# The first row of a diffusion-transformer layer on both DMA queues: when it is loaded, and what stands behind it

## The chip, the cores and the metric

The kernel runs on one core of a Trainium2 chip. Its time is the device time of one execution in microseconds (us); a run's number is compared as the median of several executions. Five engines work side by side, each in its own order and held together by semaphores: TensorE (PE: matmuls, with PEld for the loading of weights), VectorE (DVE), ScalarE (ACT), GpSimd (POOL) and SyncE (SP). SyncE and ScalarE issue nearly all transfers, each on a queue of its own (q1 and q10 in the profile).

## What is computed

One layer of a diffusion transformer on 1024 latent tokens of 1024 channels, with 256 context tokens. It begins by making the modulation from the condition vector c, and the projections read the modulated tokens:

```python
mod = jax.nn.silu(c) @ w_mod + b_mod          # 6 x 1024: shift, scale, gate for two sublayers
h   = x * (1 + scale) + shift                 # modulated latent tokens
proj = h @ w_in + b_in                        # queries, keys, values of two attentions, and gates
mixed = (sigmoid(g_a) * (o_a @ w_a) + sigmoid(g_b) * (o_b @ w_b)) @ w_out
```

The context tokens are modulated in the same way from a constant vector c_ctx. Windowed attention, global attention, the merge above and a convolutional feed-forward network follow. Everything is float32.

## The kernel before

A float32 matmul is made of three. `split` writes an operand as a high part (rounded, by ScalarE, line 80) and a low part (the difference, line 85, by VectorE or GpSimd), and `mm3` adds high times high (L88), high times low (L89 or L90) and low times high. For a weight w the parts are called wh and wl. `wsplit(wr, nm, le)` makes both from a raw weight tile; `le` names the engine of the low part. "q1acc" are eight accumulators of the first stage, "accqa" four of a later one.

The program is written as one sequence; a scheduler places each engine's instructions in an order that follows priorities and its own estimate of when their inputs are ready. So an edit in one place can change the order on engines elsewhere. Tiles come from rings of buffers: the raw weights have three, the split weights eight, and the large tiles of 128 x 1024 share 19 slots H0 to H18, handed out in turn by `ht` and given back by `hput`; a load into a slot waits until the one who used it before is done. Transfers signal one of eight completion semaphores in turn, so a ninth transfer waits for the first to land.

The first stage makes one set of queries. Before it, `spread(sc, c_row, 0)` broadcasts the row of c to 128 partitions (512 KB in a tile "row") and applies SiLU, giving `sc`. For each of eight k, `load1(k)` issues two tiles of modulation weights (wm, 512 KB each), a weight tile wr (256 KB) and a tile of x (xr, 512 KB) on SyncE's queue. `modulate(k)` splits the weight (whqb, wlqb), reduces each wm tile against sc on VectorE (`mod`, line 186, into a column of modc), and makes the modulated tokens hh (high) and hl (low). 24 matmuls per k follow: eight accumulators times three.

After the stage come, on TensorE, three gates g0 to g2 (48 matmuls each; their weights wg are split by ScalarE and GpSimd into whg and wlg), and then accqa: eight k of 12 matmuls with the weights wqa, split by ScalarE (whqa) and VectorE (wlqa). Between them VectorE does rotary embedding and norms for the queries of the first stage (rt1q, rt2q, Q, and the reduction of squares cvt<-sqq), and 48 further columns of modulation: each is one tile "wml" (512 KB, L648) reduced by line 186. wml47 is the first of these, then 46, 45 and so on; the first 16 use `scc`, the SiLU of the context's row, the others sc. The sigmoids of the gates leave through tiles sg (L666) and transfers on ScalarE's queue (L667); these tiles share the H slots with wml.

Of the kernel before, what the change touches and what calls it, by code (L numbers as in the profile page):

```python
# [13 lines left out]
P = 128  # L14
D = 1024
T = 1024
# [11 lines left out]
HALF = 512  # L28
# [39 lines left out]
def layer_kernel(  # L68
# [6 lines left out]
    nc = tc.nc  # L75
    PSUM = bass.MemoryType.PSUM

    def split(src, hi, lo, hi_eng, lo_eng):
        if hi_eng is nc.scalar:
            nc.scalar.copy(hi, src)  # L80
        elif hi_eng is nc.gpsimd:
            nc.gpsimd.tensor_scalar(out=hi, in0=src, scalar1=1.0, scalar2=0.0, op0=ALU.mult, op1=ALU.add)  # L82
        else:
            hi_eng.tensor_copy(hi, src)
        lo_eng.tensor_tensor(out=lo, in0=src, in1=hi.bitcast(F32), op=ALU.subtract)  # L85

    def mm3(ps, a, b, start, stop, resumed=False):
        nc.tensor.matmul(ps, a[0], b[0], start=start, stop=False, skip_group_check=resumed)  # L88
        nc.tensor.matmul(ps, a[0], b[1], start=False, stop=False, skip_group_check=resumed)  # L89
        nc.tensor.matmul(ps, a[1], b[0], start=False, stop=stop, skip_group_check=resumed)  # L90
# [3 lines left out]
    def ctile(shape, dt, name):  # L94
        return const.tile(shape, dt, tag=name, name=name)
# [2 lines left out]
    identr = ctile([P, P], R32, "identr")  # L98
    modc = ctile([P, 48], F32, "modc")
    bmc = ctile([P, 48], F32, "bmc")  # L100
    nc.scalar.dma_start(bmc, bmod)
    modx = ctile([P, 16], F32, "modx")
    negsink = ctile([P, 8], F32, "negsink")
    sinkb = ctile([P, 8], F32, "sinkb")
# [26 lines left out]
    def ht(name, shape=(P, T), dt=F32):  # L131
        hslot[name] = pool, tag = hfree.pop(0)
        return pool.tile(list(shape), dt, tag=tag, name=name, bufs=1)

    def hput(*names):
        for n in names:
            hfree.append(hslot.pop(n))
# [18 lines left out]
    def raw(name):  # L156
        return ph1.tile([P, 512], F32, tag="raw", name=name, bufs=RAWB)

    def wsplit(wr, nm, le="vector"):
        wh = ph1.tile([P, 512], R32, tag="wp", name=f"wh{nm}", bufs=8)  # L160
        wl = ph1.tile([P, 512], R32, tag="wp", name=f"wl{nm}", bufs=8)
        split(wr, wh, wl, nc.scalar, getattr(nc, le))
        return wh, wl
# [7 lines left out]

    sc, scc = ht("sc"), ht("scc")

    def spread(dst, src, n):
        row = ht(f"row{n}")
        hput(f"row{n}")
        nc.scalar.dma_start(row, src.partition_broadcast(P))
        nc.scalar.activation(dst, row, AF.Silu)

    def tmp(name):  # L180
        t = ht(name)
        hput(name)
        return t

    def mod(w, row, bias, o):
        nc.vector.tensor_tensor_reduce(out=w, in0=w, in1=row, scale=1.0, scalar=bias, op0=ALU.mult, op1=ALU.add,  # L186
                                       accum_out=o)
# [5 lines left out]
    def load1(k):  # L193
        wm = []
        for j in (0, 1):
            w = tmp(f"wm{j}_{k}")
            nc.sync.dma_start(w, wmodT[j * 8 + k])
            wm.append(w)
        x = tmp(f"xr{k}")
        wr = raw(f"wr{k}")  # L200
        nc.sync.dma_start(wr, w_qb[k])
        nc.sync.dma_start(x, xT[k])
        st1[k] = wm, x, wr

    def modulate(k):
        wm, x, wr = st1.pop(k)
        w = wsplit(wr, f"qb{k}")
        for j in (0, 1):
            col = j * 8 + k
            mod(wm[j], sc, bmc[:, col:col + 1], modc[:, col:col + 1])  # L210
        hh = hTp.tile([P, T], R32, tag="hT", name=f"hh{k}", bufs=16)
        hl = hTp.tile([P, T], R32, tag="hT", name=f"hl{k}", bufs=16)
        a, b = modc[:, k:k + 1], modc[:, 8 + k:9 + k]
        for s in [slice(0, HALF), slice(HALF, T)] if k == 0 else [slice(0, T)]:
            nc.scalar.activation(hh[:, s], x[:, s], AF.Identity, bias=a, scale=b)
            nc.scalar.activation(x[:, s], x[:, s], AF.Identity, bias=a, scale=b)
            nc.vector.tensor_tensor(out=hl[:, s], in0=x[:, s], in1=hh[:, s].bitcast(F32), op=ALU.subtract)
        hT.append((hh, hl))
        return w

    spread(sc, c_row, 0)
    load1(0)
    nc.vector.tensor_scalar(out=bmc[:, 8:16], in0=bmc[:, 8:16], scalar1=1.0, scalar2=None, op0=ALU.add)
    for k in (1, 2):
        load1(k)
    acc = [acc_tile(f"q1acc{t}") for t in range(NT)]
    w = modulate(0)
    for k in range(KT):
        if k == 2:
            spread(scc, cc_row, 1)  # L230
        if k + 3 < KT:
            load1(k + 3)
        wn = modulate(k + 1) if k + 1 < KT else None
        for t in range(NT):
            s = slice(t * P, (t + 1) * P)
            mm3(acc[t], (hT[k][0][:, s], hT[k][1][:, s]), w, k == 0, k == KT - 1)
        w = wn
# [461 lines left out]
    for n, (gi, k) in enumerate(order):  # L699
# [9 lines left out]
        nm, src, tiles = groups[gi]  # L709
# [3 lines left out]
        w, c = ready.pop((gi, k))  # L713
        for t in tiles:
            if t < NT:
                s = slice(t * P, (t + 1) * P)
                a = hT[k][0][:, s], hT[k][1][:, s]
            else:
                s = slice((t - NT) * P, (t - NT + 1) * P)
# [222 lines left out]
    for f in range(2, KT):  # L942
        bT[1, f] = ht(f"bT1_{f}")
        nc.sync.dma_start(bT[1, f], sgd[KT + f])
        w = wb[f // 2]
        ps = big(f"b1_{f}")
        for j in range(4):
            k = (f % 2) * 4 + j
# [588 lines left out]
    s = LN2_S[-1]  # L1537
    w = s.stop - s.start
# [207 lines left out]
```

## Time and profile before

| | |
|---|---|
| runs of the kernel (us) | 1590.85, 1590.62, 1592.18; median 1590.85 |
| profiled execution | 1593.3 us, of which the span is 1591.5 |
| mean granted clock of TensorE | 0.993 |
| TensorE busy | 1537.1 us (97%) |
| VectorE, ScalarE, GpSimd busy | 1181.3, 813.3, 730.1 us |
| traffic | 230.00 MB, mean 145 GB/s |

One execution is recorded instruction by instruction. A row of a timeline gives start, duration, engine, line, operation, "out<-in" by tile names, and in brackets how long the engine was idle before and what released it. A table of waits gives the total, the count and the longest. A row of a window gives for each engine the busy time in it, then the granted clock, the share of the DMA engines that was busy, and GB/s.

### The profile page before, as it was taken

How to read it: one execution, taken by the hardware profiler on the slowest of the kernel's cores; microseconds unless marked ns; L12 is line 12 of the kernel's file. 1: busy time of each engine (PE TensorE's matmuls, PEld its weight loads, DVE VectorE, ACT ScalarE, POOL GpSimd, SP SyncE). 2: the span in 40 equal slices, each digit the busy share in tenths (PEclk: the TensorE clock that was granted, in tenths of full speed). 3: DMA queues.
4: the chain of work that ended last, by engine and by line, in shares of the span. 5: the costliest groups of instructions: out<-in, count | busy, mean ns of one | idle time of the engine just before them, and what ended most of it. 6: DMA issues, size and time to landing. Idle time of an engine off the chain costs nothing.

```text
span 1591.5 us, 22189 instructions
## 1 busy us (share of the span) xinstructions
PE 1537.1 (97%) x7748; PEld 1278.4 (80%) x7748; DVE 1181.3 (74%) x1768; ACT 813.3 (51%) x1450; POOL 730.1 (46%) x727
## 2 busy tenths in 40 slices
PE   6999999999999999999999999999999999999997
PEld 5878788878886887777688888888888888888887
DVE  7797646628888777888674778788888788657884
ACT  5422122448888667688521564454444444535552
POOL 0573212426666556665422453566667665021021
PEclk9999999999999999999999999999999999999999
DMA  9685663322227555532451222333334446996731
GB/s 379 218 309 177 214 204 101 118 79 74 64 81 178 136 127 127 125 84 41 141 173 65 80 80 93 106 106 106 106 106 108 117 116 175 368 274 202 260 107 54
DMA packets 112368, 230.00 MB, mean 145 GB/s; under 512 B 12960, under 2 KB 27808, under 8 KB 112160
## 3 DMA queue, kind: packets, MB, share of 16 engines
q1 hardware_dynamic: 96816, 198.93, 37.9%
q0 software_dynamic: 10400, 20.19, 8.3%
q10 hardware_dynamic: 5040, 9.46, 1.6%
q8 instruction: 61, 1.00, 0.3%
q14 instruction: 51, 0.42, 0.1%
HBM read 177.35 MB, written 65.86 MB: 153 GB/s over the span
## 4 chain that ended last, share of the span: by engine, by line
PE 76%; DVE 8%; DMA 7%; ACT 4%; issue 3%; POOL 2%; SPq 0%; DVEq 0%; ACTq 0%; POOLq 0%
PE ptr L529 4%; PE p L89 3%; PE p L88 3%; PE p L90 3%; PE b L90 3%; PE b L89 3%; PE b L88 3%; PE g L88 2%; PE g L89 2%; PE g L90 2%; PE d L89 2%; PE c L89 2%; PE a L89 2%; PE c L90 2%; PE a L90 2%
## 5 line engine op out<-in xcount | busy, mean ns | idle before, releaser
L539 DVE TENSOR_TENSOR ptl<-ptr,pth 128x512 fp32r<-128x512 f32 x188 | 124.7, 685 | 28.2 <-ACT pth L538 25.8
L529 PE MATMUL ptr<-ident,p 128*128 128x128 f32 x816 | 126.6, 278 | 9.5 <-DVE ptl L539 6.9
L538 ACT CAST pth<-ptr 128x512 fp32r<-128x512 f32 x188 | 106.6, 588 | 56.3 <-PE ptr L529 32.6
L85 DVE TENSOR_TENSOR ld<-rd,hd 128x1024 fp32r<-128x1024 f32 x77 | 94.8, 1249 | 50.8 <-ACT hd L80 48.7
L424 ACT ACTIVATE p<-p,nm 128x1024 f32<-128x1024 f32 (+2 forms) x128 | 125.3, 981 | 11.2 <-DVE p L457 10.5
L529 PEld LDWEIGHTS ptr<-ident,p 128*128 128x128 f32 x816 | 93.7, 140 | 39.8 <-DVE ptl L539 13.5
L80 ACT CAST hd<-rd 128x1024 fp32r<-128x1024 f32 x77 | 79.4, 1049 | 81.9 <-PE p L90 55.5
L550 PE MATMUL av<-pth,VT 128*128 128x512 f32 x236 | 104.6, 443 | 1.0 <-ACT avs L556 0.5
L88 PE MATMUL p<-hd 128*128 128x512 f32 x264 | 103.2, 391 | 0.0
L89 PE MATMUL p<-ld,hd 128*128 128x512 f32 x264 | 102.8, 390 | 0.2 <-DVE ld L85 0.2
L90 PE MATMUL p<-hd,ld 128*128 128x512 f32 x264 | 102.7, 389 | 0.0
L88 PE MATMUL g<-hh,whg 128*128 128x512 f32 x256 | 99.9, 390 | 0.0
L90 PE MATMUL g<-hh,wlg 128*128 128x512 f32 x256 | 99.7, 389 | 0.0
L89 PE MATMUL g<-hl,whg 128*128 128x512 f32 x256 | 99.6, 389 | 0.0
L551 PE MATMUL av<-ptl,VT 128*128 128x512 f32 x236 | 97.6, 414 | 2.0 <-POOL ptl L85 1.9
L85 POOL TENSOR_TENSOR wlg<-wg,whg 128x512 fp32r<-128x512 f32 x32 | 45.5, 1428 | 113.3 <-ACT whg L80 83.1
L457 DVE TENSOR_SCALAR_CACHE_REDUCE p<-s,cvt,nmc 128x1024 f32<-128x1024 f32 x64 | 84.5, 1340 | 12.3 <-PE s L413 11.8
L412 PE MATMUL s<-KL,q 128*128 128x512 f32 (+2 forms) x192 | 76.0, 396 | 2.9 <-ACT p_x L424 2.0
L186 DVE CUSTOM_DVE_ANT_0 wml<-wml,sc,bmc 128x1024 f32<-128x1024 f32 x32 | 44.6, 1406 | 43.0 <-DMA wml<-in_wmodT_dram 40.0
L413 PE MATMUL s<-KL,q 128*128 128x512 f32 (+2 forms) x192 | 71.7, 373 | 0.0
L82 POOL TENSOR_SCALAR pth<-prw 128x512 fp32r<-128x512 f32 x48 | 31.1, 648 | 87.6 <-ACT prw L535 62.1
L80 ACT CAST wS<-s 128x512 fp32r<-128x512 f32 x76 | 45.5, 621 | 45.6 <-POOL s L1077 42.8
(420 smaller groups left out, 4959.4 us busy)
## 6 DMA issues: line engine op xcount, KB each, us to landing
wml<-in_wmodT_dram SPq DMA_DIRECT2D x48, 512.0 KB
ru<-in_w_up_dram SPq DMA_DIRECT2D x38, 512.0 KB
rd<-td SPq DMA_DIRECT2D x55, 256.0 KB
rd<-sd SPq DMA_DIRECT2D x44, 256.0 KB
rd<-in_w_dn_dram SPq DMA_DIRECT2D x33, 256.0 KB
wm<-in_wmodT_dram SPq DMA_DIRECT2D x16, 512.0 KB
wg<-in_w_g_dram SPq DMA_DIRECT2D x32, 256.0 KB
sgd<-sg ACTq DMA_DIRECT2D x32, 256.0 KB
```

What stands on the lines that cost most here:

```text
L80: nc.scalar.copy(hi, src)
L85: lo_eng.tensor_tensor(out=lo, in0=src, in1=hi.bitcast(F32), op=ALU.subtract)
L88: nc.tensor.matmul(ps, a[0], b[0], start=start, stop=False, skip_group_check=resumed)
L89: nc.tensor.matmul(ps, a[0], b[1], start=False, stop=False, skip_group_check=resumed)
L90: nc.tensor.matmul(ps, a[1], b[0], start=False, stop=stop, skip_group_check=resumed)
L424: nc.scalar.activation(p, s, AF.Exp, bias=nm[:, h:h + 1], scale=scale, accum_out=sm[:, h:h + 1])
L457: nc.vector.tensor_scalar(out=p, in0=o, scalar1=self.qscale(nqs)[:, hs] if self.br else -1.0, scalar2=self.other[:, hs], op0=ALU.mult, op1 ...
L529: nc.tensor.transpose(tr[:, h * P:(h + 1) * P], self.pslice(h, n), ident)
L538: nc.scalar.copy(hi, tr)
L539: nc.vector.tensor_tensor(out=lo, in0=tr, in1=hi.bitcast(F32), op=ALU.subtract)
L550: nc.tensor.matmul(self.av, v, hi, start=first, stop=False)
L551: nc.tensor.matmul(self.av, v, lo, start=False, stop=self.left == 0)
```

## The change

- The row of c is loaded as two halves of 64 partitions, one on ScalarE's queue and one on SyncE's, and both come first on their queues. The small tile bmc (24 KB) is issued behind it; before, it came first.
- The low part of the first weight tile (wlqb of k = 0) is made by GpSimd, no longer by VectorE.
- The first tile of x is loaded as two halves of 512 columns.
- The context's row, and with it scc, moves from k = 2 on ScalarE's queue to k = 5 on SyncE's, behind the last `load1`.

```diff
-    nc.scalar.dma_start(bmc, bmod)
...
-    def spread(dst, src, n):
+    def spread(dst, src, n, engs):
         row = ht(f"row{n}")
         hput(f"row{n}")
-        nc.scalar.dma_start(row, src.partition_broadcast(P))
+        for m, eng in enumerate(engs):
+            w = P // len(engs)
+            eng.dma_start(row[m * w:(m + 1) * w], src.partition_broadcast(w))
         nc.scalar.activation(dst, row, AF.Silu)
...
-        nc.sync.dma_start(x, xT[k])
+        for s in [slice(0, HALF), slice(HALF, T)] if k == 0 else [slice(0, T)]:
+            nc.sync.dma_start(x[:, s], xT[k][:, s])
...
-        w = wsplit(wr, f"qb{k}")
+        w = wsplit(wr, f"qb{k}", "gpsimd" if k == 0 else "vector")
...
-    spread(sc, c_row, 0)
+    spread(sc, c_row, 0, (nc.scalar, nc.sync))
+    nc.scalar.dma_start(bmc, bmod)
     load1(0)
...
-        if k == 2:
-            spread(scc, cc_row, 1)
         if k + 3 < KT:
             load1(k + 3)
+        if k == 5:
+            spread(scc, cc_row, 1, (nc.sync,))
```

ScalarE at the start of the program, before and then after, with what each instruction waits for (DMAHW0 to 7 are the completion semaphores; row_145 and row_144 are the row of c):

```order
1 L101 DMA bmc<-in_bmod_dram 128x48
2 L177 DMA row_145<-in_c_row_dram 128x1024
3 L178 ACT_TABLE_LOAD
4 L178 ACTIVATE sc<-row_145 128x1024 [waits DMAHW2_49]
5 L80 CAST whqb_181<-wr_153 128x512 [waits DMAHW4_49]
```
```order
1 L178 DMA row_144<-in_c_row_dram 64x1024
2 L224 DMA bmc<-in_bmod_dram 128x48
3 L179 ACT_TABLE_LOAD [waits DMAHW1_49]
4 L179 ACTIVATE sc<-row_144 128x1024 [waits DMAHW0_49]
5 L80 CAST whqb_183<-wr_154 128x512 [waits DMAHW5_49]
```

The load of the activation table waited for nothing; now it waits for the half of the row that SyncE issues.

GpSimd after the first stage, before and after (wlg_0 and wlg_1 here are the two halves of the third gate's low weights; rt1q, rt2q and Q are rotary steps of one query tile, tbq small tables for them):

```order
26 L85 TENSOR_TENSOR wlg_0_640<-wg_0_637,whg_0_639 128x512
27 L261 TENSOR_TENSOR rt1q_2_870<-Q_2_528,tbq_812 128x512
28 L85 TENSOR_TENSOR wlg_1_646<-wg_1_643,whg_1_645 128x512
29 L267 TENSOR_TENSOR rt2q_2_871<-Q_2_528,tbq_812 128x16x16 x2
30 L269 TENSOR_TENSOR Q_2_528<-rt1q_2_870,rt2q_2_871 128x512
31 L272 TENSOR_TENSOR tbq_981<-ropet,gcol 128x64
```
```order
27 L85 TENSOR_TENSOR wlg_0_642<-wg_0_639,whg_0_641 128x512
28 L264 TENSOR_TENSOR rt1q_2_872<-Q_2_530,tbq_814 128x512
29 L270 TENSOR_TENSOR rt2q_2_873<-Q_2_530,tbq_814 128x16x16 x2
30 L272 TENSOR_TENSOR Q_2_530<-rt1q_2_872,rt2q_2_873 128x512
31 L275 TENSOR_TENSOR tbq_983<-ropet,gcol 128x64
32 L280 TENSOR_TENSOR tbq_983<-ropet,gcol 128x2x16 x2
33 L85 TENSOR_TENSOR wlg_1_648<-wg_1_645,whg_1_647 128x512
```

The second half of the split moves behind rt2q, Q and a tbq. It reads the raw tile whose ring place wqa2 takes next.

VectorE around wlqa2, the low weights for the third k of accqa, before and after (wlqa_824 and wlqa_826 are wlqa2; wml_1078 and wml_1080 are wml33, wml_1014 and wml_1016 are wml35):

```order
116 L283 TENSOR_REDUCE cvt<-sqq 128x8
117 L269 TENSOR_TENSOR Q_4_531<-rt1q_4_975,rt2q_4_976 128x512
118 L284 TENSOR_SCALAR cvt<-cvt 128x8
119 L186 ISA wml_1078,modx<-wml_1078,scc,bmc 128x1024
120 L186 ISA modx 128x1
121 L85 TENSOR_TENSOR wlqa_824<-wqa_821,whqa_823 128x512
122 L186 ISA wml_1014,modx<-wml_1014,scc,bmc 128x1024
```
```order
114 L286 TENSOR_REDUCE cvt<-sqq 128x8
115 L272 TENSOR_TENSOR Q_4_533<-rt1q_4_977,rt2q_4_978 128x512
116 L287 TENSOR_SCALAR cvt<-cvt 128x8
117 L187 ISA wml_1080,modx<-wml_1080,scc,bmc 128x1024
118 L187 ISA modx 128x1
119 L286 TENSOR_REDUCE cvt<-sqq 128x8
120 L187 ISA wml_1016,modx<-wml_1016,scc,bmc 128x1024
121 L187 ISA modx 128x1
122 L85 TENSOR_TENSOR wlqa_826<-wqa_823,whqa_825 128x512
```

A reduction and wml35 now stand ahead of wlqa2. In the same stretch, on SyncE, wml42 moves ahead of the second wqa transfer and wml39 stays behind the third; in the first stage the low-part matmuls (L90) of each k move back, in k = 7 the first five accumulators' stand behind the eleventh matmul; on ScalarE the transfer of the gate half sgd1_1 moves behind a square and whqa1. After accqa the orders are alike.

## The prediction

> **What bounds the kernel now.** I read the page first, then the TensorE waits, then the timeline of the first 110 us, because the change touches nothing later than that. The first part of the page:
>
> ```profile
> PE 1537.1 (97%) x7748; PEld 1278.4 (80%) x7748; DVE 1181.3 (74%) x1768; ACT 813.3 (51%) x1450; POOL 730.1 (46%) x727
> ```
>
> TensorE is busy for 97% of the span, and its order of matmuls after the first stage is unchanged. So the change can only move stretches in which TensorE stands still or runs slowly. Two lie within reach. The first is the start, in the waits of TensorE (total, times, longest):
>
> ```profile
> PE q1acc L88 <- ACT hh L215: 12.8, 1, 12.8
> ```
>
> The second is in TensorE's timeline (start, duration, what, and in brackets the idle time before with its releaser), with two stretches of the table of windows (the granted clock stands after the x-counts) under it:
>
> ```profile
> 91.58 0.39 PE L88 MATMUL accqa<-whqa,hh 128*128 128x512 f32 x1
> ...
> 96.79 0.39 PE L90 MATMUL accqa<-whqa,hl 128*128 128x512 f32 x1
> 98.97 0.49 PE L88 MATMUL accqa<-whqa,hh 128*128 128x512 f32 x1 [1.79 <-ACT whqa L80]
> 101.36 0.79 PE L89 MATMUL accqa<-wlqa,hh 128*128 128x512 f32 x1 [1.90 <-DVE wlqa L85]
> ...
> 106.65 0.48 PE L89 MATMUL accqa<-wlqa,hh 128*128 128x512 f32 x1
> ```
> ```profile
> 60.00:100.00 40.00, 37.68 (x166) 30.64 (x164) 34.19 (x56) 12.79 (x20) 36.90 (x35) 1.00 0.78 273
> 100.00:110.00 10.00, 8.64 (x27) 6.91 (x28) 10.00 (x21) 1.89 (x4) 5.37 (x4) 0.66 0.87 280
> ```
>
> From 91.58 to 96.79 are 24 matmuls at full clock, so one follows another every 5.21 / 23 = 0.227 us. The third k of accqa is due at 97.02. It gets its high weights (whqa2) at 98.97, its low weights (wlqa2) at 101.36, and runs cold until 106.65, where the clock in 100:110 is 0.66. The matmul at 106.65 is the 14th of this k, due at 97.02 + 13 x 0.227 = 99.97: the place costs 6.7 us. The matmuls ahead of it have only to be done before wlqa2 is there, so a head start counts only if wlqa2 moves with it. That is the question of this case.
>
> **The change part by part.** *The start.* The row of c lands last of what SiLU needs; these are two pieces of the chain of waits, the opening of the timeline, and three 1-us windows of DMA traffic (last column GB/s):
>
> ```profile
> 1.17 6.50 DMA row<-in_c_row_dram
> 7.69 1.06 ACT sc L178
> ```
> ```profile
> 0.73 0.41 ACTq L101 DMA_DIRECT2D bmc<-in_bmod_dram  x1
> ...
> 1.66 1.28 ACT L178 ACT_TABLE_LOAD   x1 [1.66 <-PEq L1736]
> ...
> 4.68 0.17 DVE L223 TENSOR_SCALAR bmc<-bmc 128x8 f32<-128x8 f32 x1 [3.64 <-DMA bmc<-in_bmod_dram]
> ...
> 8.78 1.28 DVE L186 CUSTOM_DVE_ANT_0 wm<-wm,sc,bmc 128x1024 f32<-128x1024 f32 x1 [3.93 <-ACT sc L178]
> ...
> 9.99 0.69 DVE L85 TENSOR_TENSOR wlqb<-wr,whqb 128x512 fp32r<-128x512 f32 x1
> ...
> 11.92 1.52 ACT L215 ACTIVATE hh<-xr,modc 128x512 fp32r<-128x512 f32 x2 [2.66 <-DVE modc L186]
> 12.79 0.29 PEld L88 LDWEIGHTS q1acc<-whqb,hh 128*128 128x128 f32 x1 [12.79 <-ACT hh L215]
> ```
> ```profile
> 1.00:2.00 1.00, 0.00 (x0) 0.00 (x0) 0.04 (x2) 0.34 (x1) 0.00 (x0) 1.00 0.41 74
> 2.00:3.00 1.00, 0.00 (x0) 0.00 (x0) 0.00 (x0) 0.94 (x1) 0.00 (x0) 1.00 0.70 203
> 3.00:4.00 1.00, 0.00 (x0) 0.00 (x0) 0.00 (x0) 0.00 (x0) 0.00 (x0) 1.00 1.05 411
> ```
>
> By 3.0 us 0.28 MB have moved and by 4.0 us 0.69 MB. With both halves of the row (0.52 MB) first on both queues its bytes are out by about 3.6. The nearest row for a landing is bmc: issued first at 0.73, seen at 4.68. I take 4.7 for the row, between 4.0 (bytes plus 0.4) and 6.2 (half the gain lost). The order of ScalarE now has the wait for SyncE's half ahead of the table load, whose 1.28 us were free at 1.66 and now come behind the landing. So sc starts at 4.7 + 1.28 = 6.0 instead of 7.69. The first reduction followed 1.09 later (8.78 - 7.69), so at 7.1. Then hh followed at 11.92, 3.14 after it, with wlqb0 between; GpSimd takes this subtraction, 0.69, off VectorE, which leaves 2.45. hh starts at 9.6 instead of 11.92: TensorE leads by 2.3 us. The bounds are 3.0 (row at 4.0) and 0.8 (row at 6.2). On GpSimd the subtraction is this group of the page:
>
> ```profile
> L85 POOL TENSOR_TENSOR wlg<-wg,whg 128x512 fp32r<-128x512 f32 x32 | 45.5, 1428 | 113.3 <-ACT whg L80 83.1
> ```
>
> whqb0 follows sc on ScalarE, at about 8, so wlqb0 is done by about 10.2, before the second matmul wants it; I cost it at nothing, and at most the 0.7 by which 1.43 exceeds 0.69 if whqb0 comes late.
>
> Does the second queue help? The traffic of 1 to 8 us by queue (packets, MB, share of the engines):
>
> ```profile
> q1 hardware_dynamic: 494, 1.56, 63.1%
> q10 hardware_dynamic: 288, 0.55, 23.9%
> ```
>
> ScalarE's queue (q10) had a third of what SyncE's took, and the row crept along beside the weights. What I count is therefore that no weights stand ahead of it, not a second path. [...]
>
> By 8.0 us 1.56 + 0.55 = 2.11 MB had moved; row, bias, two weight tiles, w_qb and the first half of x are 2.12 MB, so this half is there by 9 and costs nothing. The context's row goes behind the last loads of the stage. Before, it cost SyncE a wait (total, times, longest):
>
> ```profile
> SPq L197 <- DMA row<-in_cc_row_dram: 4.8, 1, 4.8
> ```
>
> That goes, without gain, since TensorE has no wait in the stage after its first. At its new place it is issued ahead of the gate weights, which are there at 57; scc is wanted only after the additions that end at 59.8 (next rows). I cost it at nothing; uncovered it would be its 1.06 on ScalarE.
>
> *The end of the first stage.* Timeline:
>
> ```profile
> 54.38 5.45 DVE L299 TENSOR_TENSOR Q<-q1acc,bias_qb 128x512 f32<-128x512 f32 x8 [5.32 <-PE q1acc L90]
> ...
> 57.00 3.80 POOL L85 TENSOR_TENSOR wlg<-wg,whg 128x512 fp32r<-128x512 f32 x3 [5.16 <-ACT whg L80]
> ...
> 59.39 0.39 PE L90 MATMUL g<-hh,wlg 128*128 128x512 f32 x1
> ```
>
> VectorE empties the first accumulator after its third matmul of k = 7. In the new order that accumulator's last matmul is the 12th, 9 x 0.227 = 2.0 later, so the work behind it starts at 54.38 - 2.3 + 2.0 = 54.1. VectorE catches up a little (it no longer waits between accumulators: 8 x 0.6, as 97.07 and 97.67 follow each other further down, instead of 5.45), so it leads by 0.9; ScalarE and GpSimd lead by 0.3. The first low gate weights are then ready at 57.0 - 0.3 + 1.43 = 58.1, while TensorE wants them at 59.39 - 2.3 = 57.1. One us goes here: TensorE's lead is 1.3.
>
> *The weights of accqa.* On GpSimd the last gate split moves behind the work that stood after it; wqa2, on SyncE's queue, waits for that split's buffer:
>
> ```profile
> 76.13 1.30 POOL L85 TENSOR_TENSOR wlg<-wg,whg 128x512 fp32r<-128x512 f32 x1
> 77.38 1.44 POOL L267 TENSOR_TENSOR rt2q<-Q,tbq 128x256 f32<-128x256 f32 x2
> ...
> 81.74 0.33 POOL L272 TENSOR_TENSOR tbq<-ropet,gcol 128x64 f32<-128x64 f32 x1
> ```
> ```profile
> 77.46 0.33 SPq L626 DMA_DIRECT2D wqa<-in_w_qa_dram  x1
> ```
>
> Three steps from 77.38 to 81.74 now come first, 4.4 us; with the lead of 0.3 wqa2 is issued at 77.46 + 4.4 - 0.3 = 81.5, and wml39 behind it at 81.9. Against that, wml42 is issued before this wait. VectorE's timeline there, with its last steps before wlqa2, and two landings from the chain:
>
> ```profile
> 78.65 1.28 DVE L186 CUSTOM_DVE_ANT_0 wml<-wml,scc,bmc 128x1024 f32<-128x1024 f32 x1 [1.86 <-DMA wml<-in_wmodT_dram]
> ...
> 81.69 1.46 DVE L186 CUSTOM_DVE_ANT_0 wml<-wml,scc,bmc 128x1024 f32<-128x1024 f32 x1 [1.75 <-DMA wml<-in_wmodT_dram]
> ...
> 97.07 0.67 DVE L283 TENSOR_REDUCE cvt<-sqq 128x8 f32<-128x512 f32 x1
> 97.67 0.67 DVE L269 TENSOR_TENSOR Q<-rt1q,rt2q 128x512 f32<-128x512 f32 x1
> ...
> 99.42 1.27 DVE L186 CUSTOM_DVE_ANT_0 wml<-wml,scc,bmc 128x1024 f32<-128x1024 f32 x1
> 100.62 0.68 DVE L85 TENSOR_TENSOR wlqa<-wqa,whqa 128x512 fp32r<-128x512 f32 x1
> ```
> ```profile
> 78.06 5.14 DMA sgd<-sg
> ...
> 86.44 6.47 DMA wml<-in_wmodT_dram
> ```
>
> wml42's wait of 1.86 goes; wml39, landing 5.14 after its issue, is used at 87.0. From there VectorE has up to the reduction that frees the squares: five mods (1.2 each, as from 99.42 to 100.62), six short steps (0.6 each) and two rt2q (0.7 if alone, 2.4 as the trace has them), 10.3 to 12.0 us, so until 97.3 to 99.0. The old reduction ended at about 97.7 and wlqa2 at 101.3, 3.6 later. Now one more reduction (0.6) and wml35 (1.2) stand between them. From the short end, 97.3, VectorE's own work ends wlqa2 at 97.3 + 3.6 + 1.8 = 102.7. A second path ends later. wml35's transfer waits until the gate half sgd1_1 has left its buffer, and that issue now stands behind a square and whqa1 on ScalarE. The square waits for the reduction after wlqa0, at 87.0 + 1.2 + 0.6 + 1.2 + 0.6 + 0.6 = 91.2; with it, the sigmoid and the start of whqa1, some 0.7 each, the issue comes at 92.7. Landed 5.14 later, 97.8, it releases wml35, which cannot be quicker than bmc's 3.95: 101.8. With 1.2 + 0.6 wlqa2 ends at 103.6, 2.3 later than 101.30. By 6.47 for both landings it would be 107.4.
>
> **Sum.** TensorE's lead of 2.3, 1.3 after the gate weights, ends at the wait for wlqa2, which is 2.3 later; the cold matmuls behind it cost the same as before. 1593.3 + 2.3 = 1595.6 for the profiled execution, whose time is 2.45 above the median of the runs shown; against that median 1590.85 + 2.3 = 1593.2. What can be told from no change is 0.2%, 3.2 us.
>
> **The rivals.** *Faster: VectorE comes early.* It idles 1.86 + 1.75 = 3.6 us for mods before wlqa2. If wml39 lands by about 83.5, both waits go; with the lead of 0.9 and the added 1.8, wlqa2 ends at 101.30 - 3.6 - 0.9 + 1.8 = 98.6. TensorE's second matmul of that k comes at 98.6 instead of 101.36: 2.7 lower, 1588.2. TensorE then waits 2.7 us at one place instead of 1.79 + 1.90; if the clock stays up as well, the cold loss of 106.65 - 101.36 - 12 x 0.227 = 2.6 goes too, 1585.6. [...] For this rival: VectorE is busy for only 34.19 of the 40 us in 60:100, and these waits are over half of its idle time. Against: wml39 is not issued before GpSimd is through with three steps. It decides at a landing of wml39 before 85. Chance 0.23.
>
> *Slower: wml35 lands late.* The second path with the long landings, 6.47 each, puts wlqa2 at 107.4: 6.1 later, 1597.0; with one of them long, 4.8 or so, 1595.6. For it: the traffic in 60:100 is 273 GB/s at a share of 0.78. Against: little is queued behind 95 us. It decides when wml35 lands after 102.7, where the loss passes 3.2. Chance 0.22.
>
> *The row does not come earlier.* If a second queue saves nothing but the issue, the row is there at 7.69 again and the table load follows: hh 1.28 - 0.69 = 0.6 us behind the old start, and everything after it 2.9 later than in my sum. wlqa2 then ends by 106.5: 5.2 later, 1596.1. [...]
>
> **How the numbers follow.** My forecast has the remaining 0.47: 0.34 within 0.2%, 0.10 above and 0.03 below. The faster rival gives 0.14 below (clock up, or wlqa2 half a us earlier still) and 0.09 within; the two slower ones 0.28 above and 0.02 within. Faster 0.17, same 0.45, slower 0.38. The range reaches from 1587.0, within the faster rival, to 1597.0, the late landing.
>
> **What would show it.** The table load behind the row, at 4 to 6 us; the first matmul at 10.0 to 12.0; the third gate matmul waiting about 1 us for wlg; wqa2 issued at 81 to 82; VectorE waiting for wml39 until about 87; wml35 with a wait just ahead of wlqa2; and the second matmul of accqa's third k at 102.7 or later. If that matmul starts before 101.36, the prediction is wrong.

## The result and the profile after

The changed kernel took 1597.03 us (median of 7 executions, 1594.11 to 1599.92), the kernel before 1590.85 (7 executions beside it, 1590.16 to 1592.56). The ratio is 1.0035, 95% interval 1.0023 to 1.0047: slower by about 5.6 us (3.7 to 7.5), and so beyond the 0.2% that can be told from no change. The prediction had 1593.2 and a range to 1597.0; its sign is right, its size too small, and the measured median stands 0.03 above the end of the range. By its own chances slower (0.38) was less likely than no change within 0.2% (0.45). The profiled execution of the changed kernel took 1595.2, of which the span is 1593.1, at a mean granted clock of 0.993.

The engines' totals on the page of the changed kernel:

```profile
PE 1534.8 (96%) x7748; PEld 1275.8 (80%) x7748; DVE 1183.0 (74%) x1767; ACT 813.0 (51%) x1450; POOL 734.8 (46%) x728
```

GpSimd is busy for 4.7 us more and VectorE for 1.7, TensorE for 2.3 less: the work is the same but for one subtraction that went from VectorE to GpSimd, and the added time lies in waits. TensorE's waits in the first 200 us of the changed kernel (total, times, longest):

```profile
PE q1acc L88 <- ACT hh L217: 11.6, 1, 11.6
PE accqa L89 <- DVE wlqa L85: 4.6, 3, 3.4
PE accqa L88 <- ACT whqa L80: 3.1, 1, 3.1
PE accqb L89 <- DVE wlqb L85: 1.7, 2, 1.4
PE g L90 <- POOL wlg L85: 0.7, 1, 0.7
```

The first wait fell from 12.8 to 11.6, while the two at accqa grew from 1.9 and 1.8 to 4.6 and 3.1. TensorE's timeline of the changed kernel at four places shows how the lead turns into a lag:

```profile
56.76 0.50 PE L88 MATMUL g<-hh,whg 128*128 128x512 f32 x1
58.18 0.50 PE L90 MATMUL g<-hh,wlg 128*128 128x512 f32 x1 [0.69 <-POOL wlg L85]
100.08 0.78 PE L88 MATMUL accqa<-whqa,hh 128*128 128x512 f32 x1 [3.06 <-ACT whqa L80]
104.30 0.80 PE L89 MATMUL accqa<-wlqa,hh 128*128 128x512 f32 x1 [3.44 <-DVE wlqa L85]
121.61 0.50 PE L89 MATMUL accqa<-wlqa,hh 128*128 128x512 f32 x1 [0.58 <-DVE wlqa L85]
```

The third gate matmul is 1.21 us ahead of its place before (59.39). The second matmul of accqa's third k, which stood at 101.36, is 2.94 behind. The last row is a matmul that before had no wait:

```profile
117.64 0.39 PE L89 MATMUL accqa<-wlqa,hh 128*128 128x512 f32 x1
```

There the changed kernel is 3.97 behind. In its windows (the clock stands third from the end) the stretch of 100 to 110 stands at half speed nearly throughout (0.63 from 100.0 to 100.5, then 0.50 in every half us up to 110.0), where before had 0.66 (0.50 from 100.0 to 106.5, 0.68 in the next half us and 1.00 after it):

```profile
60.00:100.00 40.00, 36.45 (x160) 29.49 (x158) 35.89 (x55) 11.57 (x19) 34.93 (x34) 1.00 0.72 245
100.00:110.00 10.00, 6.48 (x14) 4.78 (x15) 10.00 (x19) 2.79 (x6) 6.38 (x5) 0.51 0.94 306
```

14 matmuls were done in these 10 us, against 27 before. Most of the lag is won back at the next group of accumulators, accqb. There before waited 2.8 us and this execution 1.7, and before ran cold (at half speed) for a while as well, which the window of 140 to 190 shows, in before:

```profile
140.00:190.00 50.00, 47.25 (x200) 38.08 (x199) 27.62 (x56) 12.79 (x21) 7.07 (x6) 0.97 0.69 231
```

and in the changed kernel:

```profile
140.00:190.00 50.00, 48.34 (x213) 39.34 (x212) 27.98 (x51) 11.04 (x18) 9.37 (x8) 1.00 0.67 218
```

A clock of 0.97 is 50 x 0.03 x 2 = 3 us at half speed. By 186 us the lag is 1.3, and the two spans end 1.6 apart. A further 0.3 lies outside the span (1595.2 - 1593.1 = 2.1, against 1.8); what makes it stays open.

So these two traces differ by 1.9 us, and the medians by 6.2. The profiled execution of before is a long one of its kind (1593.3, 2.45 above the median), that of the changed kernel a short one (1.8 below). The experiments show which of the two differences is the kernel's.

### The profile page after: what moved, and what is told of

Read it like the earlier page. It is cut to its first block, busy times and chain, and to the rows that moved or that the text cites. A ratio compares the mean times of both kernels' runs of the same rounds, so it can differ in the third digit from the quotient of the medians.

```text
span 1593.1 us, 22191 instructions
## 1 busy us (share of the span) xinstructions
PE 1534.8 (96%) x7748; PEld 1275.8 (80%) x7748; DVE 1183.0 (74%) x1767; ACT 813.0 (51%) x1450; POOL 734.8 (46%) x728
## 4 chain that ended last, share of the span: by engine, by line
PE 78%; DVE 9%; DMA 4%; ACT 4%; issue 3%; POOL 2%; SPq 0%; DVEq 0%; ACTq 0%; POOLq 0%
PE ptr L532 5%; PE p L89 3%; PE p L90 3%; PE p L88 3%; PE b L90 3%; PE b L89 3%; PE b L88 3%; PE g L88 3%; PE g L89 3%; PE g L90 3%; PE av L553 2%; PE s L415 2%; PE av L554 2%; PE d L88 2%; PE c L88 2%
## 5 line engine op out<-in xcount | busy, mean ns | idle before, releaser
L532 PE MATMUL ptr<-ident,p 128*128 128x128 f32 x816 | 126.5, 278 | 10.5 <-DVE ptl L542 7.8
L541 ACT CAST pth<-ptr 128x512 fp32r<-128x512 f32 x188 | 106.5, 588 | 56.1 <-PE ptr L532 32.4
L427 ACT ACTIVATE p<-p,nm 128x1024 f32<-128x1024 f32 (+2 forms) x128 | 125.3, 981 | 10.9 <-DVE p L460 10.2
L90 PE MATMUL p<-hd,ld 128*128 128x512 f32 x264 | 102.7, 389 | 0.0
L90 PE MATMUL g<-hh,wlg 128*128 128x512 f32 x256 | 99.8, 390 | 0.7 <-POOL wlg L85 0.7
```

The costliest lines, as they stand in the source:

```text
L427: nc.scalar.activation(p, s, AF.Exp, bias=nm[:, h:h + 1], scale=scale, accum_out=sm[:, h:h + 1])
L532: nc.tensor.transpose(tr[:, h * P:(h + 1) * P], self.pslice(h, n), ident)
L541: nc.scalar.copy(hi, tr)
```

## The experiments

**The theories.** Theory A: the loss lies around accqa and comes from the order of instructions, which the scheduler turned over there although the edit is in the first stage. The last split of the gate weights (wlg of k = 2, its second half, on GpSimd) moved behind other work; wqa2 waits for its buffer; and a reduction and wml35 now stand ahead of wlqa2 on VectorE. Against it theory B: one of the edits costs by itself wherever it stands (GpSimd's early subtraction, the halved x tile, the row on two queues). Theory C came up on the way: the place of tiles in memory changes the speed of matmuls.

Built with one part of the change left out, the kernels have one of two orders around accqa: that of the changed kernel, which I call the late order, or one in which the gate split comes early and wlqa2 directly behind the mod of wml33, which I call the early order. The order can be read before a kernel runs. The first four runs leave out one part each.

*Without the halves of the x tile* (early order):

```diff
-        for s in [slice(0, HALF), slice(HALF, T)] if k == 0 else [slice(0, T)]:
-            nc.sync.dma_start(x[:, s], xT[k][:, s])
+        nc.sync.dma_start(x, xT[k])
```

> The changed kernel without the halves of the first x tile: row on both queues, GpSimd's split and the late context row stay. In its order the last gate split stands ahead of GpSimd's rotary steps again and wlqa2 stands right behind wml33. Theory A (the loss is made by the order around accqa: late gate split, wml35 and a reduction ahead of wlqa2): the start keeps a lead of 2 us and wlqa2 is no later than before, so 1587 to 1589.5. Theory B (the loss comes with the edits at the start themselves, by transfers that now stand in each other's way): 1596 to 1597, as the changed kernel.

Measured: 1591.20 us, ratio 0.9998 (0.9986 to 1.0010).

*With the context's row where it was* (early order):

```diff
+        if k == 2:
+            spread(scc, cc_row, 1, (nc.scalar,))
...
-        if k == 5:
-            spread(scc, cc_row, 1, (nc.sync,))
```

> The changed kernel with the context's row back at k = 2 on ScalarE's queue; the other three edits stay. Its order around accqa is that of the run without the x halves. Theory A: 1587 to 1589.5. Theory B: 1596 to 1597, or about 1591 if the context's row alone is what costs.

Measured: 1590.94 us, ratio 1.0006 (0.9998 to 1.0015).

*With the first low weights split by VectorE again* (late order):

```diff
-        w = wsplit(wr, f"qb{k}", "gpsimd" if k == 0 else "vector")
+        w = wsplit(wr, f"qb{k}")
```

> The changed kernel with the first low weights made by VectorE again; the other three edits stay, and with them the new order around accqa. Theory A: the same late wlqa2 (about 104 us) whatever the start does, 1596 to 1598, with a start some 0.6 us later. Theory B in the form that GpSimd's split is what hurts: about 1589 to 1591.

Measured: 1596.88 us, ratio 1.0046 (1.0034 to 1.0059). TensorE's waits for accqa in this kernel, in the first 200 us:

```profile
PE accqa L89 <- DVE wlqa L85: 5.8, 4, 3.4
PE accqa L88 <- ACT whqa L80: 3.1, 1, 3.1
```

*With the row of c on one queue, behind bmc* (early order):

```diff
+    nc.scalar.dma_start(bmc, bmod)
...
-    spread(sc, c_row, 0, (nc.scalar, nc.sync))
-    nc.scalar.dma_start(bmc, bmod)
+    spread(sc, c_row, 0, (nc.scalar,))
```

> The changed kernel with the row of c on ScalarE's queue alone and behind bmc, as before; the other three edits stay. No lead from the row (TensorE starts at 12 to 13 us), and the order around accqa has the gate split early and wlqa2 behind wml33. Theory A: within 1.5 us of the kernel before, 1589 to 1592. Theory B (row edit is the cause): about 1591 as well; if GpSimd's split or the context's row is the cause: 1596.

Measured: 1591.63 us, ratio 1.0013 (1.0004 to 1.0023). TensorE's first wait was 13.2 here, so this kernel has no head start.

What follows from the four: taking away any one of three different parts brings the ratio down to 1.0013 or less, which no cost of a single part would do. The three have the early order. The one that keeps the late order, with GpSimd's early split taken out, keeps the loss and the same two waits, 3.1 and 3.4 at the longest. The early split is not the cause.

Two of the expectations missed: theory A had 1587 to 1589.5 for the kernels without the x halves and without the context's move, and they took 1591.20 and 1590.94. The early order takes the loss away, but the lead at the start, which both have, brings no gain over before. For the second of them the rival that the context's row alone costs had foreseen about 1591 too. Against it stand the two kernels without the x halves and with the row of c on one queue: they keep the context's row late and have no loss.

The next runs change the order alone. *The context's row at k = 3 instead of k = 5*, all else as changed (early order):

```diff
-        if k == 5:
+        if k == 3:
             spread(scc, cc_row, 1, (nc.sync,))
```

> The changed kernel with one number changed: the context's row is issued at k = 3 instead of k = 5, still on SyncE's queue. All edits at the start stay word for word, but the order around accqa is that of the runs without the x halves or without the context move (gate split early, wlqa2 right behind wml33). Theory A (the order around accqa is the whole loss): 1590 to 1592, as those runs, 5 to 7 us below the changed kernel, with wlqa2 ready by 100.5 us. Theory B (an edit at the start costs by itself): 1595 to 1597.

Measured: 1591.51 us, ratio 1.0010 (1.0001 to 1.0019): 5.5 us below the changed kernel in medians, 4.0 by the ratios (0.0025 x 1590; 1.6 to 6.4 by their intervals), for one number that moves one load. TensorE's timeline at the two matmuls that the changed kernel had at 104.30 and 121.61, and SyncE's issue of wqa2 ahead of them:

```profile
75.85 0.38 SPq L629 DMA_DIRECT2D wqa<-in_w_qa_dram  x1
...
97.81 0.50 PE L89 MATMUL accqa<-wlqa,hh 128*128 128x512 f32 x1 [1.85 <-DVE wlqa L85]
...
113.23 0.39 PE L89 MATMUL accqa<-wlqa,hh 128*128 128x512 f32 x1
```

Both kernels begin g0 within 0.14 us of each other (56.62 here, 56.76 changed), and this one is 6.5 us ahead at the third k and 8.4 at 113.23. The step from 6.5 to 8.4 comes from the clock and the waits: from 104.30 on the first 14 matmuls of the changed kernel follow each other by 0.43 us instead of 0.23, some 2.9 us in all, and one waits 0.58; here none runs cold between the two places, and one waits 1.15. The clock in the same window of five kernels, first before:

```profile
100.00:115.00 15.00, 13.64 (x49) 11.05 (x50) 15.00 (x28) 3.13 (x6) 9.29 (x7) 0.77 0.91 309
```

the changed kernel:

```profile
100.00:115.00 15.00, 11.48 (x36) 8.89 (x37) 15.00 (x28) 4.05 (x8) 8.98 (x6) 0.66 0.95 315
```

with the first low weights on VectorE (late order):

```profile
100.00:115.00 15.00, 8.53 (x25) 6.21 (x24) 15.00 (x26) 3.99 (x7) 9.63 (x8) 0.66 0.85 287
```

with the row on one queue (early order):

```profile
100.00:115.00 15.00, 14.77 (x65) 11.97 (x66) 14.81 (x28) 2.48 (x4) 8.69 (x7) 1.00 0.94 300
```

and with the context at k = 3 (early order):

```profile
100.00:115.00 15.00, 13.85 (x60) 10.90 (x59) 15.00 (x26) 2.93 (x5) 10.96 (x9) 1.00 0.87 298
```

A clock of 0.66 is 15 x 0.34 x 2 = 10.2 us at half speed, 0.77 is 6.9, and 1.00 none; in the two kernels not shown here, without the x halves and with the context where it was, it was 0.89, 3.3 us. The order alone doesn't set it. The kernel with the gate split on VectorE and the changed kernel with an early table load, both below, have 0.77, and the second of them has the late order. Nor is all of it lost: while TensorE waits, half speed costs nothing, and the wait of 3.44 lies within the 10.2 us of the changed kernel.

After accqa the kernel with the context at k = 3 gives some back, since it waits 3.9 us in accqb:

```profile
PE accqb L89 <- DVE wlqb L85: 3.9, 3, 1.7
PE accqa L89 <- DVE wlqa L85: 3.0, 2, 1.9
```

What stays is 4.1 at the end of the span (1593.1 - 1589.0). That agrees with the measured 4.0 to 5.5.

*The gate split alone*: in the changed kernel, one low part moved from GpSimd to VectorE. In the order that results wml35 still stands ahead of wlqa2, and the reduction behind it again.

```diff
-                hs.append(wsplit(wr, f"g{k}_{a}", "gpsimd"))
+                hs.append(wsplit(wr, f"g{k}_{a}", "vector" if (k, a) == (2, 1) else "gpsimd"))
```

> The changed kernel with the second low half of the third gate's weights made by VectorE instead of GpSimd, so that its raw buffer is free at about 75 us and wqa2 and wml39 are issued some 6 us earlier; wml35 stays ahead of wlqa2. Theory A1 (the late gate split is the main part): VectorE's wait of 2.6 us for wml39 goes, wlqa2 is ready at about 101, and the time is 1592 to 1593.5. Theory A2 (wml35 and its transfer behind sgd1_1 are the main part): wlqa2 stays at 103.5 to 104.5 and the time at 1596.

Measured: 1592.39 us, ratio 1.0007 (0.9997 to 1.0018); one of its eleven executions took 6421.5, the others 1588.7 to 1594.84. Its timeline:

```profile
73.28 1.79 DVE L85 TENSOR_TENSOR wlg<-wg,whg 128x512 fp32r<-128x512 f32 x1
...
75.82 0.37 SPq L629 DMA_DIRECT2D wqa<-in_w_qa_dram  x1
...
101.29 0.69 DVE L85 TENSOR_TENSOR wlqa<-wqa,whqa 128x512 fp32r<-128x512 f32 x1
...
102.03 0.79 PE L89 MATMUL accqa<-wlqa,hh 128*128 128x512 f32 x1 [3.61 <-DVE wlqa L85]
```

The split is done early, wqa2 is issued at 75.82 instead of 82.14, and wlqa2 starts at 101.29 instead of 103.56. By the ratios that takes 0.0028 x 1590 = 4.5 us off the changed kernel (1.9 to 7.0 by their intervals), and the ratio is near those of the kernels with the early order. So the late gate split, through the issue of wqa2 and of the loads queued behind it, is by the times the main part of the loss. The traced execution, 2.1 above the median of its kernel, shows less: its matmul at 102.03 is 2.27 ahead of the changed kernel's, where with the context at k = 3 it was 6.5. In the 2.3 us at wlqa2 is the reduction's 0.6, which went back behind. What the rest of the late order costs (wml35, and the early context tile below) is within the uncertainty of these ratios.

*The start, further.* SiLU's table load waits behind the row (it starts at 5.79 in the changed kernel). Two runs did a SiLU of a constant first, so that the table is there when the row lands, once with the context at k = 3 and once on the changed kernel:

```diff
+    warm = const.tile([P, 1], F32, tag="warm", name="warm")
+    nc.scalar.activation(warm, onec, AF.Silu)
```

> The previous kernel with a SiLU of one column of ones ahead of the row's, so that the activation table is loaded at about 1 us while the row is in flight. The row's SiLU then starts as soon as the row is there: TensorE's start 0.8 to 1.28 us earlier (10.3 to 10.8 us). If a lead is kept in this order, the time is about 1 us below the kernel with the context's row at k = 3; if the lead is taken away at the gate weights or at wlqa2 in this order too, no difference.

> The changed kernel, order around accqa as it is, with the early table load. Theory A: TensorE starts up to 1.28 us earlier, and this is lost at the wait for wlqa2, which hangs on VectorE, GpSimd and transfers: the time is that of the changed kernel, 1596 to 1597, and wlqa2 is ready at 103.5 to 104.5 again. Rival (wlqa2 moves with the start): 1595 to 1596, and wlqa2 at about 103.

Measured: 1605.49 us, ratio 1.0089 (1.0072 to 1.0105), and 1610.85, ratio 1.0127 (1.0111 to 1.0144). TensorE's first wait fell as meant, from 11.2 to 10.9 and from 11.6 to 11.0, yet both kernels lost some 14 us, and both expectations (about 1 us below 1591.5 or level with it; 1596 to 1597) missed by as much. The loss lies far from the edit: matmul by matmul, the first of the two falls behind the kernel with the context at k = 3 from about 980 us on, by some 1.8 us in each 80; of the 16 us between the two traces 4.7 have come up by then. By theory C the new tile of 4 bytes for each partition moves the tiles allotted after it. Two runs tell the instruction from the tile. *The same early SiLU into a tile that was there already*, with the context at k = 3:

```diff
+    nc.scalar.activation(negsink[:, 0:1], onec, AF.Silu)
```

> The kernel with the context's row at k = 3 and the early SiLU of one column, but written into a column of a constant tile that is there already, so that no tile moves in memory. In the two runs with the early table load the matmuls of the second half followed each other by some 2% more slowly, from one end to the other, which put 14 us on them. Theory C (the new column of 4 bytes moved every later tile to other addresses, and matmuls read those more slowly): the slope goes, the mean matmul of the feed-forward stage is 389 ns again and the time is 1590 to 1592. Rival (the early table load itself, or what it does to ScalarE, makes it): 1604 to 1606.

*And before with nothing but an unread tile*:

```diff
+    pad = ctile([P, 1], F32, "pad")
+    nc.vector.memset(pad, 1.0)
```

> The kernel before with one more constant column of 4 bytes, set once and never read. Orders are those of the kernel before. Theory C: matmuls of the second half slow down by some 2% and the time rises to 1600 to 1606. Rival: no change, 1590 to 1591.

Measured: 1591.41 us, ratio 1.0003 (0.9995 to 1.0012), with the first wait at 10.5; and 1606.05, ratio 1.0095 (1.0081 to 1.0109). The instruction costs nothing, the four bytes cost 15 us. One group of matmuls between 1000 and 1300 us (busy time, mean ns), with a window, in before:

```profile
L88 PE MATMUL a<-B,wA 128*128 128x512 f32 x127 | 49.4, 389 | 0.0
...
1100.00:1300.00 200.00, 200.00 (x884) 165.64 (x884) 168.88 (x154) 95.81 (x137) 135.81 (x79) 1.00 0.41 113
```

and in before with four bytes:

```profile
L88 PE MATMUL a<-B,wA 128*128 128x512 f32 x124 | 49.0, 395 | 0.0
...
1100.00:1300.00 200.00, 200.00 (x865) 162.10 (x864) 172.40 (x150) 93.45 (x133) 139.38 (x78) 1.00 0.38 109
```

The window has TensorE busy throughout and the clock at 1.00 in both, yet 865 matmuls instead of 884: 2.2% more time from one matmul to the next. This is not part of the change under study, whose matmuls keep their 389 ns; it decides how an experiment on this kernel must be made.

*Where the head start goes.* With the early order and the table early, TensorE begins g0 2.1 us ahead of before, and the median is level with it (1.0003). It waits 3.7 us for wlqa and 2.9 for wlqb on the way, low parts that VectorE makes behind mods whose weights come by transfer. So GpSimd was given those of accqb, once on the kernel of the previous experiment (early SiLU, context at k = 3) and once on before alone:

```diff
-        ready[gi, k] = wsplit(wr, f"{nm}{k}"), c
+        ready[gi, k] = wsplit(wr, f"{nm}{k}", "gpsimd" if gi == 3 else "vector"), c
```

> The kernel of the previous run with the low parts of the weights of accqb, the third projection, made by GpSimd, which stands nearly idle from 140 to 170 us, instead of VectorE, where they stand behind modulation reductions that wait for transfers. If the leads of the reordered kernels are taken away at accqb (2 to 4 us of waits for wlqb), TensorE has no such wait here and the time is 2 to 4 us below the run before: 1586.5 to 1589. If GpSimd is too slow for it (1.43 us for each against 2.7 us of matmuls), the waits come back as waits for GpSimd and the time stays at 1590 to 1592.

> The kernel before with that one edit at accqb and nothing else. It tells how much of the previous run is due to accqb alone: if the waits for wlqb there (2.8 us and a cold stretch) are all that it removes, 1586.5 to 1589; the run before should then be below it by what the head start is worth, up to 2 us.

Measured: 1586.55 us, ratio 0.9979 (0.9970 to 0.9988), and 1587.57, ratio 0.9977 (0.9967 to 0.9986). Both beat the kernel before, by 3.3 and 3.7 us. In the second, TensorE's waits of 140 to 200 us are gone, and the group of GpSimd that replaces VectorE's is

```profile
L85 POOL TENSOR_TENSOR wlqb<-wqb,whqb 128x512 fp32r<-128x512 f32 x8 | 11.6, 1456 | 15.0 <-ACT whqb L80 14.9
```

Twice as slow for each as VectorE's 0.69, it idles 14.9 us for whqb and for nothing else; in before, VectorE's mods, which stand ahead of these low parts, wait 19.9 us for their transfers in the same window. In the first kernel two waits are left there, 0.9 for wlqb and 0.4 for whqb.

The two kernels cannot be told apart, so the head start of the changed kernel is worth nothing measurable even where the order is early and accqb's low weights no longer stand behind the mods. The two traces begin g0 2.0 us apart and end level.

## Why the prediction was right, and where it was too small

**The start: right, and helped by chance.** The first rows of the changed kernel:

```profile
5.79 1.28 ACT L179 ACT_TABLE_LOAD   x1 [5.79 <-DMA row<-in_c_row_dram]
7.09 1.06 ACT L179 ACTIVATE sc<-row 128x1024 f32<-128x1024 f32 x1
8.18 1.28 DVE L187 CUSTOM_DVE_ANT_0 wm<-wm,sc,bmc 128x1024 f32<-128x1024 f32 x1 [2.08 <-ACT sc L179]
...
10.71 1.52 ACT L217 ACTIVATE hh<-xr,modc 128x512 fp32r<-128x512 f32 x2 [0.97 <-DVE modc L187]
11.58 0.79 PE L88 MATMUL q1acc<-whqb,hh 128*128 128x512 f32 x1 [11.58 <-ACT hh L217]
```

The table load comes behind the row, as foreseen. The row released it at 5.8, where 4.7 was foreseen, so sc came at 7.09 and not at 6.0, and the first matmul leads by 1.2 and not by 2.3; at g0 the lead is 2.18, and the rest of that is chance. The stage begins cold: its first 7 matmuls follow each other by 0.43 us or more and then by 0.23, where in before's profiled execution it is the first 12. In the traces of two kernels that leave this stage as before has it (four bytes; before with accqb's low parts on GpSimd) it is the first 9, and they begin g0 at 58.39 and 58.26 instead of 58.94. Against them the lead at g0 is 1.6 and 1.5. The third gate matmul waited 0.69 (foreseen: about 1), which leaves 1.21 (1.3). The rival in which the row does not come earlier (1596.1, chance 0.08) is out: it released the table load at 5.79, 1.9 us before its old 7.67. What a second queue brings by itself is not shown: what changed is also what stands ahead of the row, and no run here tells the two apart.

**The chain to wlqa2: the size 0.6 short, the path the wrong one.** GpSimd, SyncE and VectorE in the changed kernel:

```profile
79.81 2.30 POOL L85 TENSOR_TENSOR wlg<-wg,whg 128x512 fp32r<-128x512 f32 x1
...
82.14 0.33 SPq L629 DMA_DIRECT2D wqa<-in_w_qa_dram  x1
...
86.23 1.28 DVE L187 CUSTOM_DVE_ANT_0 wml<-wml,scc,bmc 128x1024 f32<-128x1024 f32 x1 [2.63 <-DMA wml<-in_wmodT_dram]
...
95.89 2.38 DVE L270 TENSOR_TENSOR rt2q<-Q,tbq 128x256 f32<-128x256 f32 x2
98.18 0.67 DVE L286 TENSOR_REDUCE cvt<-sqq 128x8 f32<-128x512 f32 x1
...
99.38 1.23 DVE L287 TENSOR_SCALAR cvt<-cvt 128x8 f32<-128x8 f32 x1
...
102.35 1.28 DVE L187 CUSTOM_DVE_ANT_0 wml<-wml,scc,bmc 128x1024 f32<-128x1024 f32 x1
103.56 0.69 DVE L85 TENSOR_TENSOR wlqa<-wqa,whqa 128x512 fp32r<-128x512 f32 x1
```

wqa2 was issued at 82.14 (foreseen 81.5), wml39 used at 86.23 (87.0), the reduction done at 98.8 (97.3 to 99.0), and wlqa2 at 104.25 (103.6). The second matmul of the third k came 2.94 late, where the sum had 2.3. But of the two paths that the prediction had to wlqa2, it named the wrong one as the later. wml35 at 102.35 shows no wait: its transfer was not the limit, and VectorE's own work was. That path had been put at 102.7 from its short end, in which the pair of rt2q had 0.7. It took 2.38, as it had in before:

```profile
94.75 2.40 DVE L267 TENSOR_TENSOR rt2q<-Q,tbq 128x256 f32<-128x256 f32 x2
```

From the reduction's end at 98.8 to wlqa2's at 104.25 it was 5.4, which is what the sum had (3.6 + 1.8), so from the long end, 99.0, this path would have given 104.4. The late-landing rival gave a time near the measured one (1597.0), but its mechanism is not what happened.

**Faster rival: out.** It needed wml39 before 85; it came at 86.23.

**A step that had no price.** The chain of waits of the changed kernel shows what stood behind the matmul at 121.61:

```profile
102.21 3.83 DMA cx<-in_ctxT_dram
...
106.12 5.77 DMA sgd<-sg
...
111.96 5.05 DMA wml<-in_wmodT_dram
...
119.86 1.70 DVE wlqa L85
...
121.61 0.50 PE accqa L89
```

A context tile is now issued at 102.21, in before at 127.6. ScalarE waits 4.9 us for its landing, the gate half behind it in that engine's order leaves late, the modulation weights that take its slot land late, and a wlqa stands behind their mod on VectorE. Here TensorE's wait was 0.58, and the lag grew by 0.7.

**The sum: the step from one execution to the median failed.** "The cold matmuls behind it cost the same as before" held within 0.3 us. The longer waits of 3.06 and 3.44 were followed by 10.2 us at half speed instead of 6.9, but the wait itself takes up 3.44 of them and 1.90 of before's; from the second matmul of the third k to the last before the wait above (120.64 against 117.41) the lag grew from 2.94 to 3.23 only, and the wait made that 3.97.

What failed is that the 2.3 was worked out against one execution of before and carried to the median unchanged. Between the two profiled executions it held (1.9 measured), and that is luck in part, since before's was itself a slow one in its first 190 us. The four bytes leave before's order as it is and slow its matmuls only much later, so that run is a second execution of before up to there. One matmul late in accqb, in before:

```profile
185.95 0.40 PE L89 MATMUL accqb<-wlqb,hh 128*128 128x512 f32 x1
```

in before with four bytes:

```profile
183.06 0.39 PE L89 MATMUL accqb<-wlqb,hh 128*128 128x512 f32 x1
```

and in the changed kernel:

```profile
187.27 0.39 PE L89 MATMUL accqb<-wlqb,hh 128*128 128x512 f32 x1
```

Against the first of these the changed kernel is 1.3 behind, against the second 4.2. The two other traces with the late order have this matmul at 189.28 (first split on VectorE) and 188.50 (early table load); without the x halves, with the context's row where it was, with the row on one queue and with the context at k = 3 it stands at 183.17, 182.81, 183.06 and 183.45. So between the late order and these early ones lie 3.8 to 6.5 us, and they are there by 186 us: that is the size of the measured loss, 3.7 to 7.5. Where before's profiled execution lost its 2.9 can be read as well: 0.55 before g0, 1.0 at accqa (the matmul at 117.64 stands at 116.13 with four bytes, and at 116.26 in before with accqb's low parts on GpSimd, which has the same order up to there), where it ran cold for 6.9 us and the kernel with four bytes for 3.3, and 1.4 in accqb, where the clock was 0.97 and 1.00. The cold time at accqa is no mark of that one execution, though, since the last-named trace has 6.9 us there too (a clock of 0.77 from 95 to 110).

How much of the loss is the clock's is not shown. The mean granted clock was 0.995 over before's 73 executions in the three later comparisons, 0.995 with the context at k = 3, 0.994 with the late order and the first split on VectorE, and 0.992 over the 7 of the changed kernel. Within before's 73 executions a clock lower by 0.001 goes with about 0.6 us more; within the changed kernel's 7 there is no such tie (0.995 in the execution of 1597.10, 0.991 in that of 1594.11). By 0.6 the difference of 0.001 to 0.003 would be 0.6 to 1.8 us of the loss. No run holds the clock and changes the order.

**What stays open.** How the loss is shared: the gate split has 4.5 of 5.6 by the ratios, with intervals wider than the rest, and less in its one trace (185.85 for the matmul late in accqb); wml35 and the context tile have what is left. Where the last of the lead goes in the kernel with both an early start and accqb's low parts on GpSimd: its two waits in accqb take 1.3 of 2.0, and near 945 us it runs cold (a clock of 0.83 from 935 to 955) where before with the same low parts does not (1.00 from 935 to 960); for the rest there is no one wait to name. And how the four bytes make the matmuls slow: no trace here shows addresses.

## What to carry to other kernels

Before costing an edit at the start of a scheduled program, look for where it turns over the order later on: here one load's place decided 4 to 5.5 us at a stage nearly 70 us behind it, and the head start itself brought nothing measurable. Make a sum from a trace against what the kernel usually does, not against its one profiled execution, above all where that execution shows a cold clock; a second trace, or the mean clock of several executions, tells which it is. A kernel that differs only far behind the place in question can serve as that second trace. And ask for each weight's split behind which waits it stands on its engine: eight splits moved from a fast engine behind transfers (VectorE, 0.69 us each) to a slow one that was free (GpSimd, 1.46) gained 0.23% with one word.

## What the runs showed of the hardware

Four bytes allotted ahead of the later tiles of before made its matmuls from about 980 us on 2.2% slower (884 to 865 in 200 us at a clock of 1.00; 389 to 395 ns for one in the group shown), 15 us in all, with the same instructions but for the one that sets the four bytes. An experiment that adds a tile measures this as well as what it is meant to.

The cold stretches at accqa have lengths of about 3.3, 6.9 and 10.2 us by the windows, the longer two near twice and three times the shortest, or they are missing, in kernels with the same work. What sets these lengths is not shown. No execution has a mean clock below 0.990, but for the one of 6421.5 us (0.231). Yet over before's 73 executions it lies between 0.992 and 0.998, and at 0.6 us for each 0.001 this goes with some 3.6 us, two thirds of the 5.6 that were to be measured.
